# Rotary table steps moved behind the splits of the first feature weights, positions requested on SP between rows 2 and 3

## The chip, the cores and the metric

The kernel runs on one core of one Trainium2 chip. Times are device microseconds of one execution, from runs on the chip; lower is better. The core has five engines that run their own instruction streams in order: TensorE (PE, with its weight loads shown as PEld), VectorE (DVE), ScalarE (ACT), GpSimd (POOL) and SyncE (SP). SP, ACT and POOL also issue DMAs.

## The reference

A hybrid decoder layer on x of 512 tokens by 1024 features, all in float32. One input projection gives queries, keys and values for retention heads (rq, rk, rv and a gate rg) and attention heads (aq, ak, av), and an indexer's queries, key and head weights (iq, ik, iw). Queries and keys of all three, the indexer's too, are rotated by tables of cosines and sines of position times frequency:

```python
inv_freq = ROPE_THETA ** (-jnp.arange(0, d, 2, dtype=jnp.float32) / d)
ang = positions.astype(jnp.float32)[..., None] * inv_freq
cos, sin = jnp.cos(ang), jnp.sin(ang)
out = jnp.concatenate([x1 * cos - x2 * sin, x1 * sin + x2 * cos], axis=-1)
```

The indexer scores every key for every token, `sum_h w[t,h] relu(q_idx[t,h] . k_idx[s])`, and the 128 best admissible keys per token are the only ones that the attention heads see. Retention and attention outputs go through one output projection, a residual and a layer norm; then come a SwiGLU feed-forward of hidden width 2816, a residual and a second layer norm.

## The kernel before

**Split operands.** TensorE multiplies in fp32r, which keeps fewer bits than float32. Each large operand is therefore split in a high part (a cast to fp32r) and a low part (the operand less its high part), and each product is three matmuls: high times high, high times low, low times high (`mm3`, lines 93 to 96). `split` (lines 85 to 91) casts on ScalarE and subtracts on VectorE; or, where its first argument is None, it writes the negated operand on ScalarE and lets a DMA on POOL's queue accumulate onto it.

**Order.** Instructions go to their engines in the order of the program text (a manual schedule). Each engine works through its own list; an instruction that waits holds up all behind it on its engine or queue.

**Stage 0, the index projection** (lines 200 to 227). The contraction over 1024 features has eight rows kt of 128. For each, SP loads the weights `w0r[kt]` and the transposed input `xr[kt]` (256 KB each, lines 114 to 116), both are split (row 0 with both halves on VectorE), and twelve matmuls of 128 by 384 add to four PSUM banks `acc0_1` to `acc0_4` (iq of tokens 128 and up). Row 7 is followed by the split of `wkr`, the small weights of ik and iw with some spare columns, and by 24 matmuls `wk` into `acc0_0`. The first three raw feature weights, 1 MB each, are requested at row 5 (`fetch(3)`).

**The rotary tables** (`rotary_tables`, lines 134 to 179) are a generator of six steps. Steps one to five are 19 small VectorE instructions on 128 by 256 elements: position times frequency, and a range reduction by several multiples of two pi. Step six is ScalarE's Abs, a load of the Sin table and four Sin, then eight DMAs of 64 KB on the queues of POOL, SP and ScalarE in turn (the indexer's tables CI and SI), and four of 128 KB on SP (CT and ST for the heads). Steps one to five are issued after rows 0 to 4, step six after row 7 (line 223). Columns (frequencies and constants) and positions, which step one needs, are requested on ScalarE's queue ahead of everything else (lines 110 to 113).

**Feature weights.** `prepare` (line 298) fetches raw weights ahead and splits half of one, 128 by 1024; three raw buffers hold two halves each, and four buffers hold high and low parts of stage 0's row weights, wk and the prepared weights in turn. Weight 0 is cast on VectorE (line 307); the first two weights are prepared ahead of the projections (lines 614 and 615). Weights 0, 1 and all even ones of this part have their low half from VectorE, odd ones from the third on from ScalarE and POOL. `weight` keeps three prepared ahead.

**Feature projections** (`proj_feature`, lines 351 to 361): sixteen of 24 matmuls of 128 by 512 (ak, aq, rk, rq), named `pf`, with four PSUM banks in turn, one of them `acc0_0` at first. Each bank is evacuated by `rope`: three VectorE instructions and an addition on POOL.

**Beside them** runs a side list, paced by costs written out by hand (`pace`, line 436): `index_rope` (lines 251 to 296), then the indexer's `logits` and `topk`. `index_rope` copies `acc0_0` on ScalarE (`iwr`), rotates the key and four pairs of heads on VectorE, rounds them on ScalarE, takes the low parts `ql` on POOL, and moves these with POOL DMAs into `qa` and `qb`, two pairs of heads at a time (lines 271 to 275). `logits(1)` then takes the heads in turn: heads 0 to 3 read the first two pairs, head 4 is the first that reads the second two. Its matmuls (lines 407 and 408) stand among those of the feature projections in TensorE's list.

After these follow the token projections with retention and attention, the output projection, and the feed-forward, which the change doesn't touch.

Of the kernel before, what the change touches and what calls it, by code (L numbers as in the profile page):

```python
# [9 lines left out]
F32 = mybir.dt.float32  # L10
# [3 lines left out]
ALU = mybir.AluOpType  # L14
# [4 lines left out]
KT = D // P  # L19
# [34 lines left out]
def hybrid_layer_kernel(ctx: ExitStack, tc: tile.TileContext, xT, x, pos, w0, wf, wt, wo,  # L54
                        wgu, wd, gng, lmg, lmb, lfg, lfb, ident_d, cols_d, masks_d, decay_d, out):
    nc = tc.nc
    V, A, G, T = nc.vector, nc.scalar, nc.gpsimd, nc.tensor
# [15 lines left out]
    def tmp(name, dt=F32):  # L73
        return tp.tile([P, 512], dt, tag="t", name=name)
# [4 lines left out]
    def dma(dst, src):  # L79
        nc.sync.dma_start(dst, src)  # L80

    def row(v, n):
        return bass.AP(tensor=v.tensor, offset=v.offset, ap=[[0, P], [1, n]])

    def split(eng_lo, hi, lo, src):
        A.copy(hi, src)  # L86
        if eng_lo is None:
            A.activation(lo, src, AF.Copy, scale=-1.0)  # L88
            nc.gpsimd.dma_start(lo.bitcast(F32), src, accum_op=ALU.add)  # L89
        else:  # L90
            eng_lo.tensor_tensor(lo, src, hi.bitcast(F32), op=ALU.subtract)  # L91
# [11 lines left out]
    cols = const.tile([P, 12], F32, name="cols")  # L103
    H = S // 2
    pos_i = tp.tile([P, S], I32, tag="t", name="pos_i")[:, :H]
# [1 line left out]
    w0r = [w0s[kt // 4][:, kt % 4] for kt in range(KT)]  # L107
    wkr = unit("s0", "wkr").rearrange("p k c -> p (k c)")[:, :KT * P]
    xr = [tmp(f"xr{kt}") for kt in range(KT)]
    nc.scalar.dma_start(cols, cols_d)  # L110
    for i in range(2):
        nc.scalar.dma_start(pos_i[64 * i:64 * i + 64],
                            bass.AP(tensor=pos.tensor, offset=pos.offset + H * i, ap=[[0, 64], [1, H]]))
    for kt in range(KT):
        dma(w0r[kt], w0[kt, :, P:])
        dma(xr[kt], xT[kt])
    KV = 456
# [64 lines left out]
    stream = [(wf[c], "VV" if c == 0 else "VQ") for c in range(8)]  # L182
# [5 lines left out]
    def fetch(n):  # L188
        while len(raws) < min(n, limit[0]):
            raws.append(wp.tile([P, 2, 1024], F32, tag="raw", name=f"raw{len(raws)}"))  # L190
            dma(raws[-1], stream[len(raws) - 1][0])
# [8 lines left out]
    tables_it = rotary_tables()  # L200
    for kt in range(KT):
        wh = wp.tile([P, S], F32R, tag="wh", bufs=4, name=f"w0h{kt}")
        wl = wp.tile([P, S], F32R, tag="wl", bufs=4, name=f"w0l{kt}")
        if kt == 0:
            V.tensor_copy(wh, w0r[kt])
            V.tensor_copy(xh[kt], xr[kt])
            V.tensor_tensor(wl, w0r[kt], wh.bitcast(F32), op=ALU.subtract)
            V.tensor_tensor(xl[kt], xr[kt], xh[kt].bitcast(F32), op=ALU.subtract)
        else:
            split(V, wh, wl, w0r[kt])  # L210
            split(V, xh[kt], xl[kt], xr[kt])
        for p, (a, b) in enumerate(((wh, xh), (wl, xh), (wh, xl))):
            for i in range(4):
                T.matmul(acc0[1 + i][:, P:], lhsT=a[:, i * P:i * P + P], rhs=b[kt][:, P:],
                         start=(kt == 0 and p == 0), stop=(kt == KT - 1 and p == 2))

        if kt == 5:
            fetch(3)
        if kt == KT - 1:
            wkh = wp.tile([P, KT * P], F32R, tag="wh", bufs=4, name="wkh")  # L220
            wkl = wp.tile([P, KT * P], F32R, tag="wl", bufs=4, name="wkl")
            split(V, wkh, wkl, wkr)
        if kt <= 4 or kt == KT - 1:
            next(tables_it)
    for kt in range(KT):
        cs = slice(kt * P, kt * P + P)
# [71 lines left out]
    def prepare():  # L298
        k = len(ready)
        if k >= 2 * limit[0]:  # L300
            return
        fetch(k // 2 + 3)
        h = wp.tile([P, 1024], F32R, tag="wh", bufs=4, name=f"wh{k}")
        l = wp.tile([P, 1024], F32R, tag="wl", bufs=4, name=f"wl{k}")
        raw = raws[k // 2][:, k % 2]
        if k == 0:
            V.tensor_copy(h, raw)
            V.tensor_tensor(l, raw, h.bitcast(F32), op=ALU.subtract)
        else:
            split(V if stream[k // 2][1][k % 2] == "V" else None, h, l, raw)  # L310
        ready.append((h, l))

    def weights_ahead():
        while len(ready) < min(taken[0] + 3, 2 * limit[0]):
            prepare()

    def weight(ahead=3):
        k = taken[0]
        taken[0] += 1
        while len(ready) < min(k + 1 + ahead, 2 * limit[0]):  # L320
            prepare()
        return ready[k]
# [8 lines left out]
    def const_loads():  # L331
        dma(ident, ident_d)
        dma(masks, masks_d)
        dma(gnb, row(gng, S))
# [63 lines left out]
    def logits(j):  # L398
        n = (j + 1) * P
        acc = score[:, j]  # L400
        qs = slice((j - 1) * P, j * P)
        prev = None
        for h in range(IH + 1):
            if h < IH:
                lp = psu(f"lg{j}_{h}")
                q = (qa, qb)[h % 2][:, h // 2, qs]
                T.matmul(lp[:, :n], lhsT=q, rhs=kh[:, :n], start=True, stop=False)
                T.matmul(lp[:, :n], lhsT=q, rhs=kl[h % 2][:, :n], start=False, stop=True)  # L408
                A.activation(lp[:, :n], lp[:, :n], AF.Relu)  # L409
            if h >= 1:  # L410
                wcol = iw[:, j, h - 1:h]
                if h == 1:
                    V.tensor_scalar(acc[:, :n], prev[:, :n], wcol, 0.0, op0=ALU.mult, op1=ALU.add)
                else:
                    V.scalar_tensor_tensor(acc[:, :n], in0=prev[:, :n], scalar=wcol, in1=acc[:, :n], op0=ALU.mult, op1=ALU.add)
            prev = lp
            yield COST[j]
        d = slice(j * P, n)
        V.tensor_tensor(acc[:, d], acc[:, d], masks[:, 0], op=ALU.add)
# [12 lines left out]
    def chain(*its):  # L432
        for it in its:
            yield from it
# [177 lines left out]


    prepare()
    prepare()
    const_loads()
    lg = chain(*[logits(j) for j in range(1, NB)])
    tk = chain(*[topk(j) for j in range(1, NB)])
# [1029 lines left out]
```

## Time and profile before

| | |
|---|---|
| median of 3 runs | 616.25 us (616.15 to 616.35) |
| profiled execution, own time | 617.05 us |
| its span in the profile | 615.3 us, 9198 instructions |
| TensorE's granted clock, mean | 0.996 of full |
| HBM read, written | 74.52 MB, 2.10 MB |
| DMA, mean over the span | 181 GB/s |

The span runs from the first instruction to the last that the profiler saw. In a row of a timeline, the first number is the start in us from the span's start, the second the duration, then engine, line of the kernel, operation, output <- inputs, their sizes and the count; a bracket tells how long the engine was idle before it, and what ended that. ACTq, SPq and POOLq (or POOL with an operation DMA) are DMA requests. In a row of DMAs the last number is the time in us from the request to the landing.

### The profile page before, as it was taken

What the parts mean: (1) busy time and instruction counts of PE and PEld (TensorE: products, weight loads), DVE (VectorE), ACT (ScalarE), POOL (GpSimd) and SP (SyncE); (2) the same over time, 40 slices, a digit from 0 to 9 for tenths busy, and PEclk for the clock granted to TensorE, in tenths of its full rate; (3) what the DMA queues carried; (4) which work ended last, traced back from release to release, by engine and by line L of the source; (5) the groups of instructions that cost most, each with busy time, mean ns of one, the idle gap of its engine ahead of it and who ended that gap; (6) DMA issues with size and microseconds to landing.
All of it is one profiled execution on the core that took longest, in us unless ns stands there. A gap on an engine that the chain in (4) does not pass through costs nothing.

```text
span 615.3 us, 9198 instructions
## 1 busy us (share of the span) xinstructions
PE 604.4 (98%) x3256; PEld 519.8 (84%) x3256; DVE 516.2 (84%) x939; ACT 350.0 (57%) x612; POOL 186.5 (30%) x203
## 2 busy tenths in 40 slices
PE   8999999999999999999999999999999999999995
PEld 6888888888888887889998888888888988887884
DVE  6888588889779977889999989898898878977856
ACT  5453355334252666787657777767777685648300
POOL 0167322431347000242003544435354321214011
PEclk9999999999999999999999999999999999999998
DMA  8987633778563683497238979798878779689602
GB/s 294 272 242 172 188 103 104 171 159 245 145 137 103 234 315 107 125 246 157 86 137 206 175 194 187 185 204 170 210 157 206 160 218 216 152 230 281 208 34 102
DMA packets 48014, 111.30 MB, mean 181 GB/s; under 512 B 8880, under 2 KB 23280, under 8 KB 42336
## 3 DMA queue, kind: packets, MB, share of 16 engines
q1 hardware_dynamic: 24784, 76.88, 37.6%
q0 software_dynamic: 22576, 33.24, 32.4%
q10 hardware_dynamic: 608, 0.60, 0.3%
q8 instruction: 25, 0.41, 0.3%
q14 instruction: 21, 0.17, 0.1%
HBM read 74.52 MB, written 2.10 MB: 125 GB/s over the span
## 4 chain that ended last, share of the span: by engine, by line
PE 80%; issue 9%; DVE 5%; DMA 4%; POOL 2%; ACT 0%; POOLq 0%; DVEq 0%; ACTq 0%; SPq 0%
PE ga L904 10%; PE ga L906 5%; PE gc L904 5%; PE pf L94 5%; PE pf L95 5%; PE pf L96 5%; PE ga L912 5%; PE gc L906 3%; PE gb L904 3%; PE mx L96 2%; PE mx L94 2%; PE mx L95 2%; PE gc L912 2%; PE pt L95 2%; PE pt L94 2%
## 5 line engine op out<-in xcount | busy, mean ns | idle before, releaser
L86 ACT CAST wh<-raw 128x1024 fp32r<-128x1024 f32 x43 | 45.1, 1051 | 52.7 <-issue 20.1
L855 POOL DMA_DIRECT2D t<-t x34 | 29.1, 857 | 88.0 <-DVE t L988 58.6
L94 PE MATMUL pf<-xh,wh 128*128 128x512 f32 x128 | 50.0, 391 | 0.0
L95 PE MATMUL pf<-xl,wh 128*128 128x512 f32 x128 | 49.9, 390 | 0.0
L96 PE MATMUL pf<-xh,wl 128*128 128x512 f32 x128 | 49.9, 390 | 0.0
L855 POOL DMA_DIRECT2D w<-w x34 | 38.9, 1155 | 30.5 <-DVE w L938 23.9
L464 POOL TENSOR_TENSOR rs<-ve,half 128x1 f32<-128x1 f32 (+1 forms) x11 | 11.8, 1072 | 103.1 <-DVE ve L463 102.9
L91 DVE TENSOR_TENSOR wl<-raw,wh 128x1024 fp32r<-128x1024 f32 x24 | 29.1, 1221 | 16.3 <-ACT wh L86 16.3
L94 PE MATMUL pt<-wh,xh 128*128 128x512 f32 (+1 forms) x96 | 38.5, 402 | 0.0
L95 PE MATMUL pt<-wl,xh 128*128 128x512 f32 (+1 forms) x96 | 37.0, 386 | 0.0
L96 PE MATMUL pt<-wh,xl 128*128 128x512 f32 (+1 forms) x96 | 36.7, 382 | 0.0
L89 POOL DMA_DIRECT2D wl<-raw x19 | 16.9, 888 | 59.2 <-ACT wl L88 52.3
L96 PEld LDWEIGHTS pf<-xh,wl 128*128 128x128 f32 x128 | 24.0, 188 | 5.1
L94 PEld LDWEIGHTS pf<-xh,wh 128*128 128x128 f32 x128 | 24.0, 188 | 4.6
L95 PEld LDWEIGHTS pf<-xl,wh 128*128 128x128 f32 x128 | 24.1, 188 | 4.6
L426 DVE MAX8 m<-score 128x8 f32<-128x256 f32 (+2 forms) x48 | 26.8, 558 | 1.1
L427 DVE MATCH_REPLACE8 score<-m,score 128x256 f32<-128x256 f32 (+2 forms) x48 | 26.0, 543 | 0.0
L409 ACT ACTIVATE lg<-lg 128x256 f32<-128x256 f32 (+2 forms) x24 | 10.9, 474 | 24.6 <-PE lg L408 22.6
L89 POOL DMA_DIRECT2D slot<-hu x9 | 10.9, 1336 | 37.9 <-ACT slot L88 37.9
L96 PEld LDWEIGHTS pt<-wh,xl 128*128 128x128 f32 x96 | 18.0, 188 | 3.4
L988 DVE TENSOR_TENSOR t<-t,gc 128x512 f32<-128x512 f32 x17 | 11.7, 688 | 10.8 <-ACT t L987 10.8
L94 PEld LDWEIGHTS pt<-wh,xh 128*128 128x128 f32 x96 | 18.1, 188 | 2.7
(1185 smaller groups left out, 1990.0 us busy)
## 6 DMA issues: line engine op xcount, KB each, us to landing
graw<-in_wgu_dram SPq DMA_DIRECT2D x22, 1024.0 KB, 5.3
wl<-raw POOLq DMA_DIRECT2D x19, 512.0 KB, 5.3
raw<-in_wf_dram SPq DMA_DIRECT2D x8, 1024.0 KB, 6.0
raw<-in_wo_dram SPq DMA_DIRECT2D x8, 1024.0 KB, 5.1
raw<-in_wt_dram SPq DMA_DIRECT2D x6, 1024.0 KB, 6.0
r<-in_wd_dram SPq DMA_DIRECT2D x12, 512.0 KB, 5.8
w<-w POOLq DMA_DIRECT2D x34, 128.0 KB, 3.7
graw<-graw POOLq DMA_DIRECT2D x17, 256.0 KB, 3.7
```

The source lines that it names most:

```text
L86: A.copy(hi, src)
L89: nc.gpsimd.dma_start(lo.bitcast(F32), src, accum_op=ALU.add)
L91: eng_lo.tensor_tensor(lo, src, hi.bitcast(F32), op=ALU.subtract)
L94: T.matmul(acc, lhsT=lh, rhs=rh, start=first, stop=False, **kw)
L95: T.matmul(acc, lhsT=lh, rhs=rl, start=False, stop=False, **kw)
L96: T.matmul(acc, lhsT=ll, rhs=rh, start=False, stop=last, **kw)
L426: V.max(m8, a)
L427: V.match_replace(out=a, in_to_replace=m8, in_values=a, imm_value=TAKEN)
L855: nc.gpsimd.dma_start(t[:, :Q], t[:, Q:], accum_op=ALU.add)
L904: T.matmul(pair, lhsT=h[:, ws[k]], rhs=parts[q][:, :, k], start=first and k == 0, stop=False, skip_group_check=True)
L906: T.matmul(full[:, :Q], lhsT=l[:, ws[k]], rhs=parts[q][:, 0, k], start=False, stop=k == 3, skip_group_check=True)
L912: T.matmul(gp[n][acc], lhsT=a[:, i * S + k * P:i * S + k * P + P], rhs=parts[q][:, b, k], start=first and j == 0, stop=j == 11, skip_group ...
```

## The change

Columns and positions are requested on SP, between rows 2 and 3, and no longer on ScalarE's queue. Table steps one and two are issued after rows 3 and 5; steps three to six after the preparation of weights 0 and 1, ahead of the constant loads and the feature projections. Weight 0 is split like the others, with its cast on ScalarE.

```diff
-    nc.scalar.dma_start(cols, cols_d)
-    for i in range(2):
-        nc.scalar.dma_start(pos_i[64 * i:64 * i + 64],
-                            bass.AP(tensor=pos.tensor, offset=pos.offset + H * i, ap=[[0, 64], [1, H]]))
     for kt in range(KT):
+        if kt == 3:
+            dma(cols, cols_d)
+            for i in range(2):
+                dma(pos_i[64 * i:64 * i + 64],
+                    bass.AP(tensor=pos.tensor, offset=pos.offset + H * i, ap=[[0, 64], [1, H]]))
         dma(w0r[kt], w0[kt, :, P:])
         dma(xr[kt], xT[kt])
...
-        if kt <= 4 or kt == KT - 1:
+        if kt in (3, 5):
             next(tables_it)
...
-        if k == 0:
-            V.tensor_copy(h, raw)
-            V.tensor_tensor(l, raw, h.bitcast(F32), op=ALU.subtract)
-        else:
-            split(V if stream[k // 2][1][k % 2] == "V" else None, h, l, raw)
+        split(V if stream[k // 2][1][k % 2] == "V" else None, h, l, raw)
         ready.append((h, l))
...
     prepare()
     prepare()
+    for _ in range(4):
+        next(tables_it)
     const_loads()
```

## The prediction

> **What bounds the kernel now.** I read the page first, then the busy time by stretches, the waits of TensorE, and last the rows of each engine in the first 75 us.
>
> ```profile
> PE 604.4 (98%) x3256; PEld 519.8 (84%) x3256; DVE 516.2 (84%) x939; ACT 350.0 (57%) x612; POOL 186.5 (30%) x203
> ```
>
> TensorE is busy for 98% of the span, so a change can gain only where TensorE waits, and a wait that it newly gets is lost at once. By stretches (us, PE busy with its count, then PEld, DVE, ACT and POOL in the first row; PE alone in the second):
>
> ```profile
> 8.29:25.58 17.29, 16.09 (x85) 14.52 (x86) 16.88 (x33) 11.44 (x19) 1.45 (x3) 1.00 0.99 314
> ```
> ```profile
> 31.06:130.00 98.94, 98.94 (x451) 1.00 0.63 165
> ```
>
> From 8.29 to 25.58, while rows 1 to 7 of the index projection are multiplied, VectorE has 16.88 of 17.29 us filled: it is the bound there. From the first feature weight (31.06) on, TensorE never waits. What TensorE waited for in the first stage, from its waits (total, times, longest):
>
> ```profile
> PEld acc L214 <- DVE w0l L91: 2.8, 5, 1.1
> ```
>
> Five times the weight load stood still for a split's low half on VectorE, 2.8 us in all. VectorE was late because five table steps stood between the splits. The PE row shows only 17.29 - 16.09 = 1.2 us idle, but the ends of matmuls are modelled and overlap; a matmul can't start without its weights, so I take the gain nearer to 2.8: **2.7 us**, with 1.2 as the low end. The first feature matmul then starts at 31.06 - 2.7 = 28.4.
>
> **The moved table steps.** Steps three to five are eight multiply-adds and four roundings on VectorE (durations in ns, min/median/max):
>
> ```profile
> L140 DVE SCALAR_TENSOR_TENSOR angles<-turns,angles x11: 418/424/426, 9.7 to 18.8; 128x256 f32<-128x256 f32 x11
> L143 DVE TENSOR_SCALAR turns<-angles x3: 294/294/296, 8.0 to 18.2; 128x256 f32<-128x256 f32 x3
> ```
>
> That is 8 x 0.424 + 4 x 0.294 = 4.6 us, which now stands behind the splits of the first two feature weights. Step six is on ScalarE (Abs, the Sin table load, four Sin), with twelve DMAs on three queues. The question is when all this is done, and who is then late. VectorE and ScalarE before:
>
> ```profile
> 22.79 1.22 DVE L91 TENSOR_TENSOR wkl<-wkr,wkh 128x1024 fp32r<-128x1024 f32 x1
> 23.92 0.69 DVE L307 CAST wh<-raw 128x1024 fp32r<-128x1024 f32 x1
> 24.64 1.23 DVE L308 TENSOR_TENSOR wl<-raw,wh 128x1024 fp32r<-128x1024 f32 x1
> 27.58 2.36 DVE L91 TENSOR_TENSOR wl<-raw,wh 128x1024 fp32r<-128x1024 f32 x2 [1.71 <-ACT wh L86]
> 33.54 0.69 DVE L233 TENSOR_TENSOR rt<-acc,tables 128x512 f32<-128x512 f32 x1 [3.60 <-ACT iwr L253]
> ...
> 56.35 0.68 DVE L235 TENSOR_TENSOR rt<-pf,tables 64x512 f32<-64x512 f32 x1
> ```
> ```profile
> 20.32 1.05 ACT L86 CAST wkh<-wkr 128x1024 fp32r<-128x1024 f32 x1 [3.13 <-DMA wkr<-in_wt_dram]
> 21.27 0.41 ACT L166 ACTIVATE angles<-angles 128x256 f32<-128x256 f32 x1
> ...
> 24.56 1.82 ACTq L174 DMA_DIRECT2D tables<-trig  x2
> 26.50 2.00 ACT L86 CAST wh<-raw 128x1024 fp32r<-128x1024 f32 x2 [1.97 <-DVE wl L308]
> 31.03 1.05 ACT L86 CAST wh<-raw 128x1024 fp32r<-128x1024 f32 x1 [2.54 <-PE acc L95]
> 31.98 1.06 ACT L88 ACTIVATE wl<-raw 128x1024 fp32r<-128x1024 f32 x1
> 32.94 0.57 ACT L253 COPY iwr<-acc 128x512 f32<-128x512 f32 x1
> ```
>
> Before, VectorE's first rotation (L233) started at 33.54, held up only by the copy iwr. From there to 57.03 its rows stand end to end, so a late start can't be made up by then. When does it start after the change? The first raw feature weights arrive here:
>
> ```profile
> 17.62 1.57 SPq L80 DMA_DIRECT2D raw<-in_wf_dram  x3
> 23.84 2.55 SPq L174 DMA_DIRECT2D tables<-trig  x3
> 26.44 6.35 SPq L80 DMA_DIRECT2D tables<-trig  x4
> ```
> ```profile
> raw<-in_wf_dram SPq DMA_DIRECT2D x1, 1024.0 KB, 5.2
> ```
>
> The first lands at 17.62 + 5.2 = 22.8. wkh and wkl are done by 20.32 + 1.05 + 1.22 = 22.6, when VectorE is no longer held by tables, so the wk matmuls, due at 25.58 - 2.7 = 22.9, are covered with 0.3 us to spare (a little more, since their third matmul is the first that needs wkl). Weight 0 is now cast on ScalarE (1.05, to 23.9) in place of VectorE's 0.69; the low halves of weights 0 and 1 end 2.36 later, at 26.2; the table steps at 30.8. Weights 0 and 1 are there before 28.4. In the trace before, Abs starts at 21.27 and ScalarE is through with step six, its two DMA issues included, at 24.56 + 1.82 = 26.38: 5.1 us. So ScalarE comes free at 35.9. **Behind the waiting Abs stand** the casts of weights 2 and 3, the negated copy of weight 3 (POOL's accumulating DMA needs it), and iwr: three pitches of 0.95 (31.03, 31.98, 32.94) bring iwr to 38.8, the rotation follows 0.6 later: 39.4, and 39.5 with the 0.1 us that each of two or three hand-overs costs (26.38 to 26.50). The start moves from 33.54 to 39.5, by **6.0 us**, while TensorE would run 2.7 earlier. Weight 2 is split by 35.9 + 1.05 + 1.22 = 38.2, and wanted two projections after 28.4, at 39.3 (one is about 5.4 us: 47.83, quoted below, less 31.06 is three of them and two matmuls): covered.
>
> The tables themselves must land by 39.5. SP issues its share from 23.84 + 9.6 = 33.4 (Abs moves by 30.8 - 21.27 = 9.6) over 2.55 us, the last near 35. Two rows bound the landing:
>
> ```profile
> tables<-trig SPq DMA_DIRECT2D x1, 64.0 KB, 8.1
> ```
> ```profile
> tables<-trig SPq DMA_DIRECT2D x1, 128.0 KB, 2.4
> ```
>
> 8.1 us was taken while raw transfers of 1 MB stood ahead; 2.4 when they had gone. After the change the three raws have landed before 33.4, so I take 2.4 to 3: about 38, covered by 1.5 us. At 8.1 it would be 43.1, 3.6 us late. SP's other four table requests, the constants and the fourth raw keep their order behind these; even at 6.35 us for the four they are out by 42.3, and that raw's weights, the seventh and eighth, are wanted only after 28.4 + 6 x 5.4 = 60.8. POOL's two small memsets now come ahead of its table requests and cost nothing there.
>
> **Who is late.** The same 6.0 us reaches whatever follows from ScalarE and VectorE. POOL's rows, and the landings of its DMAs:
>
> ```profile
> 33.34 0.95 POOL L89 DMA_DIRECT2D wl<-raw  x1 [7.23 <-ACT wl L88]
> ...
> 57.12 1.28 POOL L237 TENSOR_TENSOR akT<-rt,rt 128x512 f32<-128x512 f32 x1 [1.05 <-DVE rt L235]
> 58.39 1.01 POOL L270 TENSOR_TENSOR ql<-qs,qa 128x384 fp32r<-128x384 f32 x1
> 59.69 1.05 POOL L275 DMA_DIRECT2D qa<-ql  x2 [0.29 <-POOL ql L270]
> ```
> ```profile
> wl<-raw POOLq DMA_DIRECT2D x1, 512.0 KB, 6.4
> ```
> ```profile
> qa<-ql POOLq DMA_DIRECT2D x1, 96.0 KB, 5.9
> ```
>
> And when TensorE wants them: weight 3's low half with the third matmul of the fourth projection, the index queries of the second pair with the fifth head's weight load:
>
> ```profile
> 47.83 0.39 PE L96 MATMUL pf<-xh,wl 128*128 128x512 f32 x1
> ```
> ```profile
> 72.55 0.19 PEld L407 LDWEIGHTS lg<-kk,qa 128*128 128x128 f32 x1
> ```
>
> Weight 3 landed at 33.34 + 6.4 = 39.7; it will land at 45.7, and is wanted at 47.83 - 2.7 = 45.1. TensorE waits 0.6 there, and 2.1 us of gain are left. The second pair (second DMA of the two from 59.69, so 60.2) landed at 66.1; POOL there waits for VectorE's last back-to-back rotation (57.12 <-DVE rt L235), so it moves by the whole 6.0, to 72.1. TensorE stood at 72.55 before. So it can be there no more than 0.45 us earlier than before, **however much the first stage gained**: of 2.7 us, 2.2 are given back, 0.6 at weight 3 and 1.6 or so at this load. After it nothing is later than before.
>
> One row moves this a little. The pair shares the DMA engines with a raw transfer:
>
> ```profile
> 59.87 0.33 SPq L80 DMA_DIRECT2D raw<-in_wf_dram  x1
> ```
> ```profile
> qa<-ql POOLq DMA_DIRECT2D x1, 96.0 KB, 2.9
> ```
>
> A DMA of the first pair, with no raw ahead of it, landed in 2.9 (issued 49.5); the late one came 0.3 behind the raw and took 5.9. The raw's release came through an accumulate whose POOL issue had waited 0.55 us for ScalarE; that wait goes, so the raw starts about half a microsecond earlier against the pair, which gives the gain an end of 0.95. I take 0.5.
>
> **The moved requests.** Columns and positions took 0.41 + 1.20 us of ScalarE's queue:
>
> ```profile
> 0.74 0.41 ACTq L110 DMA_DIRECT2D cols<-in_cols_dram  x1
> 1.19 1.20 ACTq L112 DMA_DIRECT2D pos_i<-in_pos_dram  x2
> ```
>
> On SP they stand ahead of rows 3 to 7, wk and the raws, 1.6 us at most, or nothing if SP only waits for room; the DMA share of 0.99 in the first stretch says that the transfers, not their requests, set the pace. I take 0, bounds 0 and 1.6 us (below zero for rows 1 and 2, which have fewer bytes ahead). The Trainium skill (DMA: Bandwidth & Descriptors, Issuing engines are not separate DMA queues) says that DMAs of all issuing engines share the same 16 DMA engines, and that another issuer saves only issue time. By it the sum stays; the 0.99 agrees.
>
> **The sum.** -2.7 in the first stage, +0.6 at weight 3, +1.6 at the second query pair: -0.5 us. The profiled execution took 617.05 around its span of 615.3; it would take 616.5. The median of the runs, 616.25, is 0.8 below it, and becomes **615.7**.
>
> **The rivals.**
> 1. *The query pair isn't held up.* If it lands in 2.9 us instead of 5.9 it is there at 69.1, before it is wanted; weight 3 decides, and 2.1 us of gain stay: 614.1 (613.5 if that lands sooner too). For it: the 2.9 row, and ScalarE's two DMA issues (1.82) may be shorter with idle queues. Against: 5.9 was measured in just this neighbourhood. The Trainium skill (DMA: Bandwidth & Descriptors, Queues, rings and completion order) says that a DMA engine takes turns between queues packet by packet, by which a small POOL transfer need not wait out SP's raw; the rows 2.9 and 5.9 speak against it. Chance 0.37.
> 2. *The tables become the wait.* All of the index rotation stands behind the last of the eight small table DMAs. If they need the 8.1 us of before, from 35 on, the rotation starts at 43.1, the pair is 3.6 us later still, and -0.45 becomes +3.15: 619.4. It decides from a landing time of 4.5 us on, one for one, and the kernel is slower than can be told from no change from 6.2 us on. For it: twelve requests on three queues within 9 us, and the only rows of such small ones are 8.1 and its like. Against: what stood ahead of those has landed. Chance 0.09.
> 3. *The first stage gains less,* since rows arrive no faster: at 1.2 us the query pair still decides, and nothing changes in the sum. It belongs to the forecast. So do late requests: 1.6 us on SP would delay the first raw, with it the whole chain, and make +1.15 of -0.45.
>
> **How the numbers follow.** The forecast with the third rival has 0.55, rival one 0.36, rival two 0.09. About 0.2%, 1.2 us, is what can be told from no change. The forecast's ends are -0.95 and +1.15; 0.05 of its chance spills below the 1.2 and 0.03 above, while 0.02 of rival one and 0.01 of rival two lie within. So faster 0.36 - 0.02 + 0.05 = 0.39, slower 0.09 - 0.01 + 0.03 = 0.11, same 0.50. The range takes in rival one and the forecast's upper end: 613.9 to 617.4; the forecast's own is 615.3 to 617.4.
>
> **What would show it.** Right: VectorE's first rotation at 39 to 40, the waits of weight loads for w0l nearly gone, the first feature matmul near 28.4, and new waits of TensorE at weight 3 (a DMA wl<-raw) and at L407 (a DMA qa<-ql), 2.2 us together. Wrong: no wait at L407 and a gain of 2 us (rival one); tables landing after 40 (rival two); the first raw landing after 24 (late requests).

## The result, and the profile after

The changed kernel takes 620.26 us (median of 15 runs, 617.49 to 625.59) against 616.25 (15 runs, 615.57 to 617.68). The ratio is 1.0068, 95% interval 1.0047 to 1.0089: slower by 4.2 us, 2.9 to 5.5. That lies outside the range of 613.9 to 617.4. The profiled execution took 621.6 around a span of 619.8, 4.5 us more than before. The runs also spread nearly four times as far as before.

TensorE's busy time grew by 0.7 us and its idle time by 3.8, so most of the loss is in waiting. From the page, and from TensorE's waits (total, times, longest), of the changed kernel:

```profile
PE 605.1 (98%) x3256; PEld 520.9 (84%) x3256; DVE 516.7 (83%) x938; ACT 350.8 (57%) x613; POOL 186.8 (30%) x203
```
```profile
PE pf L96 <- DMA wl<-raw: 4.2, 1, 4.2
...
PE acc L96 <- DVE wkl L91: 0.5, 1, 0.5
```

The waits for w0l of the first stage are gone, as forecast. In their place stand 0.5 us for wk's low half and 0.3 for its high half (in this execution wk landed 1.1 us later than before), and one wait of 4.2 us: the third matmul of the fourth feature projection stands still for weight 3's low half. TensorE's rows around it:

```profile
45.44 0.39 PE L95 MATMUL pf<-xl,wh 128*128 128x512 f32 x1
50.05 0.79 PE L96 MATMUL pf<-xh,wl 128*128 128x512 f32 x1 [4.22 <-DMA wl<-raw]
50.64 0.63 PE L94 MATMUL pf<-xh,wh 128*128 128x512 f32 x1
51.07 0.63 PE L95 MATMUL pf<-xl,wh 128*128 128x512 f32 x1
...
55.33 0.63 PE L96 MATMUL pf<-xh,wl 128*128 128x512 f32 x1
55.76 0.43 PE L94 MATMUL pf<-xh,wh 128*128 128x512 f32 x1
```

Read the starts: behind the wait they are 0.43 us apart, where before it and from 55.76 on they are 0.23 apart. The same in the stretch behind the wait, before the change (TensorE alone) and after it (the last three numbers are the granted clock, the DMA share and GB/s):

```profile
51.00:56.00 5.00, 5.00 (x24) 1.00 0.77 252
```
```profile
51.00:56.00 5.00, 5.00 (x13) 3.86 (x12) 4.88 (x8) 1.87 (x3) 3.36 (x5) 0.52 0.96 280
```

TensorE does 13 matmuls where it did 24, at a granted clock of 0.52. The 13 pitches from 50.05 to 55.76 take 5.7 us for 13 x 0.227 = 2.95: 2.8 us on top of the wait. The feature projections as a whole, by the first and last start of their first matmuls, before and after:

```profile
L94 PE MATMUL pf<-xh,wh x128: 387/389/476, 31.1 to 126.5; 128*128 128x512 f32 x128
```
```profile
L94 PE MATMUL pf<-xh,wh x128: 387/389/628, 28.9 to 131.6; 128*128 128x512 f32 x128
```

They start 2.2 us earlier and end 5.1 later: 7.3 us are lost inside, of which the wait (4.6 from start to start, less a pitch: 4.4) and the clock make 7.2.

How weight 3 came to be late is read from three engines, VectorE, ScalarE and POOL, and two landings:

```profile
32.01 0.43 DVE L141 SCALAR_TENSOR_TENSOR angles<-turns,angles 128x256 f32<-128x256 f32 x1
...
40.95 0.69 DVE L234 TENSOR_TENSOR rt<-acc,tables 128x512 f32<-128x512 f32 x1 [1.15 <-ACT iwr L254]
```
```profile
24.12 2.00 ACT L86 CAST wh<-raw 128x1024 fp32r<-128x1024 f32 x2 [1.68 <-DMA raw<-in_wf_dram]
32.47 0.42 ACT L167 ACTIVATE angles<-angles 128x256 f32<-128x256 f32 x1 [6.35 <-DVE angles L141]
...
37.49 2.00 ACT L86 CAST wh<-raw 128x1024 fp32r<-128x1024 f32 x2 [1.77 <-issue]
39.40 1.05 ACT L88 ACTIVATE wl<-raw 128x1024 fp32r<-128x1024 f32 x1
40.35 0.56 ACT L254 COPY iwr<-acc 128x512 f32<-128x512 f32 x1
```
```profile
40.75 0.95 POOL L89 DMA_DIRECT2D wl<-raw  x1 [3.59 <-ACT wl L88]
```
```profile
raw<-in_wf_dram SPq DMA_DIRECT2D x1, 1024.0 KB, 5.9
```
```profile
wl<-raw POOLq DMA_DIRECT2D x1, 512.0 KB, 9.3
```

ScalarE stands 6.35 us at Abs for the last table step, with the casts of weights 2 and 3 and weight 3's negated copy behind it. POOL's accumulate is so issued at 40.75, where it was at 33.34, and takes 9.3 us, where it took 6.4. It lands at 50.05; TensorE wanted it at 45.7.

### The profile page after: what moved, and what is told of

It reads as the page before. It is cut to its first block, busy times and chain, and to the rows that moved or that the text cites. A ratio compares the mean times of both kernels' runs of the same rounds, so it can differ in the third digit from the quotient of the medians.

```text
span 619.8 us, 9196 instructions
## 1 busy us (share of the span) xinstructions
PE 605.1 (98%) x3256; PEld 520.9 (84%) x3256; DVE 516.7 (83%) x938; ACT 350.8 (57%) x613; POOL 186.8 (30%) x203
## 4 chain that ended last, share of the span: by engine, by line
PE 82%; DVE 5%; DMA 5%; issue 2%; ACT 1%; SPq 1%; POOL 1%; ACTq 0%; POOLq 0%; DVEq 0%
PE ga L903 10%; PE ga L905 5%; PE gc L903 5%; PE ga L911 5%; PE pf L96 4%; PE pf L95 4%; PE pf L94 4%; PE gc L905 3%; PE pt L95 3%; PE pt L94 3%; PE gb L903 3%; PE pt L96 3%; PE mx L96 2%; PE mx L94 2%; PE mx L95 2%; PE gc L911 2%
## 5 line engine op out<-in xcount | busy, mean ns | idle before, releaser
L96 PE MATMUL pf<-xh,wl 128*128 128x512 f32 x128 | 51.2, 400 | 4.2 <-DMA wl<-raw 4.2
L89 POOL DMA_DIRECT2D wl<-raw x19 | 16.9, 887 | 52.5 <-ACT wl L88 45.7
L94 PEld LDWEIGHTS pf<-xh,wh 128*128 128x128 f32 x128 | 24.8, 193 | 4.9
L406 ACT ACTIVATE lg<-lg 128x256 f32<-128x256 f32 (+2 forms) x24 | 10.9, 474 | 24.6 <-PE lg L405 22.4
```

The lines of the kernel that those rows point to most:

```text
L94: T.matmul(acc, lhsT=lh, rhs=rh, start=first, stop=False, **kw)
L96: T.matmul(acc, lhsT=ll, rhs=rh, start=False, stop=last, **kw)
```

## The experiments

**The theories.** A: the place of the late table steps. ScalarE waits in order for them, weight 3's accumulate is issued late and lands slowly, and TensorE waits, with a slow clock behind the wait. B: the requests of columns and positions on SP, which delay the raws. C: the second pair of index queries holds TensorE, as the prediction had it. Ten more kernels were run, and the changed one twice more. Each time is a median beside runs of the kernel before on the same chip; the views are of one execution each.

**Requests back on ScalarE's queue.**

```diff
+    nc.scalar.dma_start(cols, cols_d)
+    ... (both halves of the positions)
     for kt in range(KT):
-        if kt == 3:
-            dma(cols, cols_d)
...
```

> The changed kernel with columns and positions requested on ScalarE's queue again, as before the change. Theory A (TensorE's 4.2 us wait for weight 3's low half, whose accumulating DMA is issued late because ScalarE waits for the table steps, and the half clock that follows it): the first raw lands near 22.8 again and not 24.0, the accumulate is issued near 39.5, the wait shrinks by about 1.2 us but stays, near 3; 618 to 619 us. Theory B (the requests on SP are the whole loss): 615 us or less, no wait at weight 3. Theory C (the second pair of index queries holds TensorE): a wait at L404's weight load, 616 us.

619.23 us (ratio 1.0039, 1.0024 to 1.0054). The first raw landed at 22.9, the accumulate was issued at 39.51 and landed in 7.2. TensorE's wait, and its rows behind it:

```profile
PE pf L96 <- DMA wl<-raw: 2.2, 1, 2.2
```
```profile
46.77 0.50 PE L96 MATMUL pf<-xh,wl 128*128 128x512 f32 x1 [2.16 <-DMA wl<-raw]
...
48.26 0.62 PE L96 MATMUL pf<-xh,wl 128*128 128x512 f32 x1
```

As A has it, the wait is shorter but stays, and a slow stretch is still there, from 48.26 to 51.67 (the 0.62 is its first). The kernel is still slower than before without any change of the requests, so B isn't the whole loss. The two intervals (this one's and the changed kernel's) overlap: 1 us of the loss may be the requests', which the medians don't settle. The profiled execution took 617.25 us, 2 less than the median, so the wait of the median run may be longer than 2.2.

**Weight 3's low half on VectorE.**

```diff
-    stream = [(wf[c], "VV" if c == 0 else "VQ") for c in range(8)]
+    stream = [(wf[c], "VV" if c < 2 else "VQ") for c in range(8)]
```

> The changed kernel with weight 3's low half subtracted on VectorE, so that it needs no accumulating DMA. Theory A: the wait at weight 3 and the slow clock behind it go; if nothing else is late, 616.25 - 2.2 = 614 us. Theory C: then the next accumulate (weight 5, issued near 52, wanted near 56.6) and the second query pair (landed at 74.3 in the changed kernel, wanted near 70.4 once the wait is gone) hold TensorE, 3 to 4 us in all; 617 to 618 us with a wait at a weight load of lg. Theory B: no change against the changed kernel beyond noise, 620 us.

619.27 us (1.0054, 1.0032 to 1.0076). The wait at weight 3's accumulate is gone, and the gain did not come back:

```profile
PE lg L404 <- DMA qa<-ql: 2.9, 1, 2.9
PE pf L94 <- ACT wh L86: 1.3, 1, 1.3
```

The query pair now holds TensorE for 2.9 us, as C has it, and weight 2's high half for 1.3, its low half for another 0.5. That is more than the 617 to 618 us that C gave. In this execution, 1.2 us above the median, the first raw landed at 25.9, later than in the changed kernel (24.0); whether that holds for the median run isn't shown.

**The fourth raw first.**

```diff
     prepare()
     prepare()
+    fetch(4)
     for _ in range(4):
         next(tables_it)
```

> The changed kernel with the fourth raw requested ahead of the table steps, so that its 1 MB has landed before weight 3's accumulating DMA starts. Theory A with contention (the accumulate's 9.3 us come from sharing the DMA engines with that raw): it lands in 5 to 6 us, near 46, the wait at weight 3 falls below 1 us and the clock stays up; what is left is the query pair of theory C, 615 to 618 us. If contention with the raw isn't the cause, it lands in 8 to 9 us as in the changed kernel and the time stays at 619 to 621 us.

618.13 us (1.0029, 1.0017 to 1.0041). The landing of the accumulate, and the waits:

```profile
wl<-raw POOLq DMA_DIRECT2D x1, 512.0 KB, 5.6
```
```profile
PE lg L404 <- DMA qa<-ql: 2.4, 1, 2.4
...
PE pf L96 <- DMA wl<-raw: 0.7, 1, 0.7
```

With the 1 MB transfer out of its way, the accumulate needed 5.6 us, not 9.3, and the wait at weight 3 fell to 0.7, close to the 0.6 that had been forecast for the changed kernel. Then TensorE waits for the query pair, 2.4 us, and the median is still above the kernel before, just outside the 615 to 618 us that had been expected.

**Tables behind four weights.**

```diff
-    prepare()
-    prepare()
+    for _ in range(4):
+        prepare()
     for _ in range(4):
         next(tables_it)
```

> The changed kernel with the four late table steps behind the preparation of four weights, not two, so that ScalarE does weights 2 and 3 before it waits for the tables. Theory A: weight 3's accumulate is issued near 31 and lands before 40, no wait there, the first rotation starts near 39.3; what is left is up to 1.5 us for the query pair (theory C); 614.5 to 616 us. Theory B: the raws still land late, 619 us or more.

619.82 us (1.0058, 1.0042 to 1.0075): a miss. VectorE's first rotation, and TensorE's waits:

```profile
43.71 0.69 DVE L234 TENSOR_TENSOR rt<-acc,tables 128x512 f32<-128x512 f32 x1 [8.32 <-DMA tables<-trig]
```
```profile
PE lg L404 <- DMA qa<-ql: 2.3, 1, 2.3
PE pf L94 <- DVE rt L236: 2.0, 2, 1.3
PE pf L96 <- DMA wl<-raw: 1.4, 1, 1.4
```

Weight 3 is in time, but the tables are later still (the first raw landed at 25.7 here, the last step ended at 35.4), and now the landing of the tables starts the rotation, 2.7 us after iwr. TensorE waits at three places behind it: for PSUM banks that the rotation had not emptied, for weight 5's accumulate and for the query pair. The wait of ScalarE was only one way in which late tables reach TensorE.

**Only the requests moved.** The kernel before, with columns and positions on SP between rows 2 and 3 and nothing else.

> The kernel before with only the requests of columns and positions moved to SP. The four runs so far show the first raw landing at 22.8 with the requests on ScalarE's queue and at 23.6 to 25.8 with them on SP. Theory A: without the moved table steps the accumulate of weight 3 has some 8 us of cover, and 1 to 3 us less of it cost nothing: 616 to 616.8 us, no new wait of TensorE but a few tenths in the first stage. Theory B (the requests are the loss by themselves): 618 us or more.

618.92 us (1.0038, 1.0024 to 1.0052): slower, but not through the raws. VectorE in the first stage, and TensorE's wait:

```profile
9.41 0.29 DVE L147 CAST angles<-pos_i 128x256 f32<-128x256 int32 x1 [3.60 <-DMA pos_i<-in_pos_dram]
```
```profile
PE acc L215 <- DVE w0l L91: 3.1, 2, 2.6
```

Step one stands behind row 0 in this kernel; it waits 3.6 us for positions that are now behind row 2, and row 1's low half waits behind it. The first stage's granted clock falls to 0.93 as well. Behind the first stage nothing more is lost: the projections run from 33.3 to 128.7, both 2.2 us later than before, though the first raw landed at 24.6. The time is the one that B had named and A's 616 to 616.8 was missed, but late raws, B's reason, cost nothing here. So the two parts of the change belong together: with step one still behind row 0, the requests on SP cost time.

**The steps in a gap.** VectorE waits for wk between the splits of row 7 and wk's split, from 18.7 to 22.5 in the changed kernel. Steps three and four go there, step five behind wk's split, and only step six stays behind weights 0 and 1.

```diff
+            next(tables_it)
+            next(tables_it)
             split(V, wkh, wkl, wkr)
-        if kt in (3, 5):
+        if kt in (3, 5, KT - 1):
             next(tables_it)
...
     prepare()
     prepare()
-    for _ in range(4):
-        next(tables_it)
+    next(tables_it)
```

> The changed kernel with steps three and four ahead of wk's split, step five behind it and step six behind weights 0 and 1: they fill the time in which VectorE waits for wk (18.7 to 22.5). Theory A: ScalarE gets the angles by 26 instead of 32.4, weight 3's accumulate is issued near 35 and lands before 45, the first rotation starts near 35, the query pair lands near 68 and is wanted near 70.4; no wait behind the first stage, its whole gain stays: 614 to 615 us. Theory B: raws still 1 to 3 us late, 616 us or more.

614.22 us (0.9964, 0.9949 to 0.998): faster than both, by 2.2 us against the kernel before. VectorE's rows, POOL's accumulate for weight 3, and the feature projections:

```profile
18.52 0.42 DVE L141 SCALAR_TENSOR_TENSOR angles<-turns,angles 128x256 f32<-128x256 f32 x1
...
24.18 0.43 DVE L141 SCALAR_TENSOR_TENSOR angles<-turns,angles 128x256 f32<-128x256 f32 x1
...
34.06 0.69 DVE L236 TENSOR_TENSOR rt<-acc,tables 128x512 f32<-128x512 f32 x1 [1.15 <-ACT iwr L256]
```
```profile
33.86 0.95 POOL L89 DMA_DIRECT2D wl<-raw  x1 [3.57 <-ACT wl L88]
```
```profile
L94 PE MATMUL pf<-xh,wh x128: 387/389/476, 27.9 to 123.3; 128*128 128x512 f32 x128
```

The last step ends at 24.6, not 32.4; the rotation starts at 34.1, half a microsecond from where it was before; the projections start 3.2 us earlier than before and end 3.2 earlier. The accumulate of weight 3 took 9.3 us here too, but was issued 6.9 us earlier than in the changed kernel, and TensorE has no wait for it or for the query pair. The requests on SP are the same as in the changed kernel, so the place of the steps is the cause of the loss: A.

**The same, requests back on ScalarE's queue.**

> The same with the requests on ScalarE's queue again. Theory A: what is moved off the path is the same, so 614 to 615 us, within 0.5 of the one before; rows 1 and 2 land later, wk earlier. Theory B: a microsecond or more faster than with the requests on SP.

613.86 us (0.9958, 0.9945 to 0.9971), 0.4 us from the one before, intervals on top of each other. B has no part that these two can tell. The first raw landed at 24.0 in this one, so its time of landing isn't set by the requests' queue alone: over all profiles here, it was 22.7 to 24.0 with the requests on ScalarE's queue and 23.2 to 26.4 with them on SP, and the two ranges overlap. What else sets it is open.

**The wait filled.** Sixteen overwritten matmuls ahead of the fourth projection of the changed kernel:

```diff
+                            for _ in range(16):
+                                T.matmul(acc, lhsT=h[:, cs], rhs=xh[kt], start=True, stop=True)
```

> The changed kernel with sixteen more matmuls (3.6 us) on TensorE where it waits for weight 3's low half, which repeat the first one of that projection and are overwritten. If the slow clock behind the wait costs by itself (14 matmuls at 0.43 us for 0.23, 2.5 us), filling the wait keeps the clock up: 617.5 to 618.5 us, granted clock 1.00 from 46 to 56. If it is the wait alone that costs, the time stays at 620 us, or grows by what the filling exceeds the wait.

620.89 us (1.0067, 1.005 to 1.0084): not faster, where 617.5 to 618.5 had been expected if the clock costs by itself. Its feature projections:

```profile
L94 PE MATMUL pf<-xh,wh x128: 387/389/476, 30.0 to 130.0; 128*128 128x512 f32 x128
```

They take 100.0 us where the changed kernel's took 102.7, with no wait at weight 3 and a granted clock of 1.00; but they started 1.1 later, and TensorE had waited 1.1 us for an input row in the first stage. With so much scatter in its start this kernel can't settle what the clock costs. The next two, built on the kernel with the steps in the gap and the requests on ScalarE's queue, can.

**A pure wait, and the same time filled.** One kernel has a wait of TensorE built in ahead of the fourth projection (its added lines are shown), the other twenty overwritten matmuls at the same place.

```diff
+                            for _ in range(3):
+                                A.copy(acc, prev)
+                            A.copy(hop[0], acc[:, :32])
+                            nc.scalar.dma_start(hop[1], hop[0])
+                            T.matmul(acc[:32, :32], lhsT=hop[1], rhs=hop[1], start=True, stop=True)
```

> The kernel with the steps in the gap and the requests on ScalarE's queue (613.9 us, no wait at weight 3), with a wait of TensorE built in ahead of the fourth feature projection: four copies on ScalarE from the third one's bank, a DMA of 16 KB and a small matmul that reads it, all overwritten. From the rows so far that is 3 x 0.57 + 0.2 + 0.6 + 2.1, about 4.5 us. If a wait of this length also halves TensorE's clock for the next 5 to 6 us, as behind the 4.2 us of the changed kernel, it costs 4.5 + 2.5: 620.5 to 621.5 us, with a granted clock near 0.5 behind it. If a wait costs only itself: 618 to 619 us.

> The same kernel with twenty matmuls of 0.227 us, 4.5 us, at that place instead of the wait, overwritten too. If the clock is what a wait costs on top: 618 to 619 us, 2 to 3 us below the one with the wait, granted clock 1.00 throughout. If it isn't, both come out within 0.7 us.

623.21 us (1.0114, 1.0094 to 1.0134) with the wait, 619.13 (1.004, 1.0026 to 1.0054) with the filling. The wait, and the stretch behind it; then the filled kernel's stretch (PE alone):

```profile
PE pf L370 <- ACT qb L271: 5.0, 1, 5.0
```
```profile
50.00:56.00 6.00, 6.00 (x17) 0.62 0.78 226
```
```profile
50.00:56.00 6.00, 6.00 (x28) 1.00 0.76 243
```

The wait's row names a cast of ScalarE, but that had ended long before; what came last was the 16 KB DMA behind the copies, requested at 47.74 and landed 1.7 us later. The wait came out at 5.0 us, half a microsecond longer than the filling. The projections ran from 28.1 to 131.4 with it, 103.3 us, from 28.2 to 128.3 with the filling, 100.1, and from 28.5 to 124.0, 95.5, with neither (the kernel with the steps in the gap and the requests on ScalarE's queue):

```profile
L94 PE MATMUL pf<-xh,wh x128: 387/389/796, 28.1 to 131.4; 128*128 128x512 f32 x128
```
```profile
L94 PE MATMUL pf<-xh,wh x128: 387/389/476, 28.2 to 128.3; 128*128 128x512 f32 x128
```
```profile
L94 PE MATMUL pf<-xh,wh x128: 387/389/476, 28.5 to 124.0; 128*128 128x512 f32 x128
```

So 4.5 us of filling cost 4.6, and 5.0 us of waiting 7.8: the slow clock adds 2.8 us to the wait. TensorE has no other wait in the projections of either. The medians of the two, taken side by side, are 4.1 us apart, of which 0.5 is the longer wait. Against the median of the kernel with neither, which was not taken beside them, the filling is 5.3 above and the wait 9.3.

**The changed kernel twice more,** one execution each.

> The changed kernel once more, for its spread (617.5 to 625.6 us). Theory A: the time follows the wait at weight 3, which follows the landing of the first raw and of the accumulate: own time near 616.25 - 2 + wait + 2.5 if the wait is over 2 us.

> The same once more: if this execution has another time, the difference to the other two lies in the landing of the first raw, the wait at weight 3 and the slow clock behind it, within 0.7 us.

620.16 and 620.51 us. The wait at weight 3 and the accumulate's landing in the first:

```profile
PE pf L96 <- DMA wl<-raw: 5.2, 1, 5.2
```
```profile
wl<-raw POOLq DMA_DIRECT2D x1, 512.0 KB, 10.1
```

In the first the raw landed early, at 23.3, and the accumulate was issued at 39.9, but it took 10.1 us; in the second the raw came at 24.8, the accumulate was issued at 41.44 and took 9.0. The waits are 5.2 and 4.2 and the slow clock is there both times. By 616.25 - 2 + wait + 2.5 the two would take 622.0 and 621.0; they took 1.8 and 0.4 less, and the one with the longer wait was the faster. The traces show two of the reasons: in the first the projections started 0.8 us earlier (28.0 and 28.8), and the slow clock cost less than 2.5 us, 1.9 in the first (nine pitches from 50.08 to 54.07, 3.99 us for 2.04) and 1.7 in the second (eight from 50.49 to 54.02, 3.53 for 1.82).

## Why the prediction was wrong, step by step

**The first stage: right, a little large.** 2.7 us were forecast, the feature projections started 2.2 earlier (31.1 to 28.9). The rest went to wk, for which 0.3 us of cover had been named and which came 1.1 later in this execution (0.2 and 1.0 in the other two).

**The chain to the rotation: right in kind, 1.4 us short.** The table steps took 5.0 us (forecast 4.6), step six on ScalarE 5.0 (5.1), and ScalarE stood behind the last step as described. The rotation started 7.4 us later than before, not 6.0: the first raw landed at 24.0 where 22.8 had been carried over. The term for late requests had been taken as 0 from bounds of 0 and 1.6. Whether the requests made the raw late is not shown: it landed at 23.2 to 24.8 in the three executions of this kernel, and at 24.0 in one with the requests back on ScalarE's queue.

**The tables: right.** They landed 2.3 to 3.7 us after their requests, where 2.4 to 3 had been taken from the near row. The rival of late tables did not come about in the changed kernel. It did where they were moved further back.

**Weight 3: the step that failed.** "Weight 3 landed at 33.34 + 6.4 = 39.7; it will land at 45.7, and is wanted at 47.83 - 2.7 = 45.1. TensorE waits 0.6 there." It landed at 50.05. Of the error, 1.4 us is the later issue (40.75 for 39.3) and 2.9 the landing time, which was carried over from one row as if it were a constant. In that row the fourth raw had been requested 1.15 us behind the accumulate, much as after the change (0.96). In the ten profiles with the raw about 1 us behind it, the same 512 KB took 6.4 to 10.1 us, and the 6.4 of the kernel before is the low end; with the raw landed ahead of it, it took 5.6. So a raw beside it goes with a longer landing, but what makes 6.4 or 10.1 of the same order of requests stays open. The prediction gave the query pair two landing times, 2.9 and 5.9, and weight 3 only one. Its chance of 0.11 for a slower kernel stood for late tables and late requests; weight 3 was not among them.

**The clock: not in the sum at all.** A wait was priced at its own length. In the profiled execution the 4.2 us cost 2.8 more, at a granted clock of 0.52; the pair of a built-in wait and a filling of the same place puts it at 2.8 too. In the other two executions of the changed kernel it was 1.9 and 1.7. The fifteen runs of the changed kernel fall apart by it: the five with a mean granted clock of 0.996 or 0.997 took 617.5 to 619.2 us, the ten with 0.990 to 0.994 took 619.8 to 625.6. So about 2 us were lost even where the clock stayed up (the median of the five is 618.1); none of those five was profiled, so their waits aren't known.

The Trainium skill (TensorE: Matmul & The Clock Gate, HAM oscillation — how this bites in real kernels) says that a gap of TensorE over about 3.4 us sends its clock back to half. The waits of 4.2, 5.0 and 5.2 us agree with it; the 2.2 us wait with the requests moved back and the 2.6 us wait in the first stage with only the requests moved had a slow stretch behind them too, and the waits of 2.3, 2.4 and 2.9 us at the index queries had none, so here its length alone doesn't tell. At the forecast 0.6 us the clock would not have counted (the 0.7 us wait with the fourth raw first had no slow stretch); from about 2 us of wait on, by these rows, it should have stood among the rivals on the slower side.

**The query pair: right in kind, too small, and hidden.** TensorE never waited for it in the changed kernel, since it lost more at weight 3. In the three kernels in which that wait was gone or short it did, 2.3 to 2.9 us, forecast 1.6. Its DMAs, which were to move by "the whole 6.0", were issued 9.2 us later than before in the changed kernel (68.92 for 59.69) and 7.7 later with the fourth raw first (67.40). So the pair does take the gain of the first stage back while the rotation is late, but in the changed kernel weight 3 and the clock cost more than the pair would have.

**The sum.** -2.2 in the first stage, +4.4 at weight 3, +2.8 for the clock: +5.0, against the 5.1 by which the projections end later and the 4.5 of the span; behind the projections the two profiles differ by the other 0.6.

## What to carry to other kernels

Work that is moved off a busy stage goes best into an idle stretch of its own engine: here the same steps, moved into the time in which VectorE waited for wk, gave 2.2 us, and moved behind the next weights cost 4. When a step is moved that another engine waits for in order, list everything queued behind that wait, and give each DMA in the list a range of landing times, not the one of a single row: the same accumulate took 6.4 to 10.1 us with the same request behind it. A wait of TensorE of two microseconds or more has to be priced at its length and, as a risk, the half clock behind it, here 1.6 to 2.8 us where it came.

## What the runs showed of the hardware that wasn't expected

- Weight 3's accumulating DMA of 512 KB, issued from POOL, took between 4.9 and 10.1 us. It took 5.6 where the fourth raw of 1 MB had landed ahead of it, 4.9 where that had been requested 2.3 us ahead, 10.0 where it had been requested 0.07 us ahead, and 6.4 to 10.1 in the ten profiles where it was requested about 1 us behind. So a load requested later can go with a slower landing; the spread among the ten is not explained.
- The clock falls some time after TensorE's wait begins, whether or not work has resumed. After the wait of 2.2 us that ended at 46.77, TensorE ran six matmuls at full pace and only then, from 48.26, 3.4 us at the slow one, which cost 1.6 us. In the changed kernel the granted clock was already at 0.5 from 49.0, inside the wait, and stayed there for 6.8 us, to 55.8. In all six profiles with such a stretch in their first 130 us it began 2.3 to 4.3 us after the wait did and lasted 3.4 or 6.8 us, and only the part of it that falls on work costs time.
- With columns and positions behind rows 0 to 2, ScalarE's casts of row 1 started 0.9 to 1.0 us earlier in the profiled execution (weights at 5.66 for 6.60, input at 6.63 for 7.61), and 0.2 to 1.1 earlier over the three executions of the changed kernel; wk came 0.2 to 1.1 later in these, and the first raw, several transfers further on, 0.4 to 3.6 us later in the eight profiles with the requests on SP behind row 2 and the table steps moved. Between executions of the one kernel it differed by 1.6 us (23.2 to 24.8), so not all of that can be put down to the requests.
